# A mixture-of-experts block on one core: the next X loaded earlier, the experts' order turned, the branches of a last tile exchanged

## The chip, the core and the metric

The kernel runs on one NeuronCore of a Trainium2 chip, as one launch. Its engines are PE (TensorE matmul; PEld is its weight load), DVE (VectorE), ACT (ScalarE), POOL (GpSimd) and SP (SyncE, which here issues DMAs), and each takes its own list of instructions in order. The metric is device time in microseconds (us): 1101.23 us is the median of 3 runs before (1100.25 to 1102.68).

## The reference

One decoder layer over 1024 tokens of 1024 features: a gated spatial mixer and a sliding-window attention side by side, then a hierarchical mixture of experts, then a norm. The change touches the experts alone:

```python
# e_logits of the best of 4 groups; two experts of 4 inside it
combine = jnp.einsum("tk,tke->te", w_top, one_hot(expert_id, 16))
for e in range(16):
    hid = jax.nn.silu(t @ w_gate[e]) * (t @ w_up[e])      # 1024 -> 512
    out = out + combine[:, e:e+1] * (hid @ w_down[e])     # 512 -> 1024
```

Each token goes to two experts, so 2048 rows are shared out. By the reference's router on its own inputs the sixteen experts get 121, 82, 97, 130, 75, 39, 98, 76, 245, 162, 227, 134, 128, 113, 152 and 169 rows.

## The kernel before, in words

The dense part (some 648 us) ends with the routing, which writes every token's row into a queue in DRAM for each of its experts. Then the experts run one after the other, at places 0 to 15. Each matmul is made from three (high times high, high times low, low times high), so each weight must be split into a high part (ACT, L307) and a low part (DVE, L313 or L317). A granule is 128 x 1024 of raw weights, 512 KB: an expert has 12, k0 to k7 of gate and up (two DMAs of 256 KB) and k8 to k11 of down (one DMA of 512 KB). Granule g's raw buffer is loaded again with granule g + 9 when its low part is made (`load_others`, SP, L288). Fifteen split tiles go round in a ring.

An expert at place e has a main tile of its first 128 rows, and ahead of it, if it has more, a last tile: "half" (`half_tile`, up to 64 rows more) or "whole" (`whole_tile`). Both are in `last_tile` (L1574 ff.): an If on n > 128 (L1591), inside it an If on n <= 192 (L1595) with the half form, its Else with the whole one, and at the end the Else of the outer If with `fill(0)` and `fill(1)`, the first gate and up matmuls of the main tile, which in the other forms fill PE's waits. Places 0 and 15 have the whole form alone. All engines pass these branches, and tokens' counts are read at run time.

While PE works on the main tile of place e, ACT and DVE split granules of e + 1 at named steps (`ahead`, by the tables AHEAD_0 for e = 0, AHEAD_1 for e = 1, AHEAD for the others): "h5 l5" is high and low of granule k5. The steps of a main tile: ("k", 0 to 3) both halves of gate and up; ("f0", 5); then the first half's hidden rows (`hidden(0)`: Silu on ACT, L1388, product on DVE, L1389); ("f1", 5); their transposes on PE (`hidden_T`, L1395, which PE reaches in order) and the copies (L184 ACT, L185 DVE); ("f1", 7); the down projection (L1433) with ("y", 0), ("y", 1), ("y", 2) between its four steps. At ("y", 1) PE transposes the next expert's rows, X (L1344, from the buffer `xt_first`), and POOL copies their tail (L1337). At ("y", 2) SP loads X of place e + 2 into the same buffer (`first_rows`, L1328). At ("k", 2) SP loads the last rows of e + 1 (`last_rows`, L1475 to L1480, buffer `xt_last`; skipped where n does not ask for them, but issued).

SP and POOL run in the written order (`manual_schedule`). SP's order at the end of an expert is so that of the code in `ahead`: the loads that the lows of a step set off, then X. For places e > 1, ("y", 2) has one low, l11, which loads the next but one expert's k8; for e = 1 it has three, and for e = 0 seven.

`RANK_AT[p]` says which rank by count stands at place p (places 0 and 1 are fixed experts, the rest is sorted by `order_experts`). Before, the counts by place are 121, 82, 130, 128, 134, 113, 152, 98, 162, 97, 169, 76, 227, 75, 39, 245. With N for no last tile, H for half and W for whole, that is N N H N H N H N H N H N W N N W, which the trace shows in the tiles' names (2h, 4h, 6h, 8h, 10h, 12l, 15l). The last one's W is in the tail, which isn't changed.

Of the kernel before, what the change touches and what calls it, by code (L numbers as in the profile page):

```python
# [20 lines left out]
P = 128  # L21
H = P // 2
# [10 lines left out]
NE = 16  # L33
# [33 lines left out]

ORDER_AT = ("y", 2)

RANK_AT = [0, 1, 8, 9, 7, 10, 6, 11, 5, 12, 4, 13, 3, 14, 15, 2]  # L70

WARM = 42
WARM_ROUTE = 10
# [20 lines left out]
def kernel(  # L94
# [71 lines left out]
    def slot8(shape, dt, name):  # L166
        return slots.tile(shape, dt, tag="s8", name=name)

    def ps_mm(name):
        return ps.tile([P, 512], F32, tag="mm", bufs=4, name=name)  # L170

    def ps_tp(name):
        return ps.tile([P, 512], F32, tag="tp", bufs=2, name=name)
# [7 lines left out]
    def split_hi_lo(hi, lo, src, scale=None):  # L181

        if scale is None:
            nc.scalar.activation(hi, src, AF.Copy)  # L184
            return nc.vector.tensor_tensor(lo, src, hi, ALU.subtract)  # L185
        nc.scalar.activation(hi, src, AF.Copy, scale=scale)
        return nc.vector.scalar_tensor_tensor(lo, src, scale, hi, ALU.mult, ALU.subtract)
# [56 lines left out]
    def first_row(p):  # L244

        if p == len(first_rows_of):
            first_rows_of.append(
                nc.values_load(
                    base_i[0:1, p : p + 1], engines=[mybir.EngineType.SP],
                    min_val=0, max_val=(NE - 1) * CAP,  # L250
                )
            )
        return first_rows_of[p]

    class Granules:
# [63 lines left out]
        def fill(self, g):  # L319
            self.high(g)  # L320
            self.low(g)
# [1003 lines left out]
    def load_x(src, name, xt=None, **kw):  # L1325
        if xt is None:
            xt = moe.tile([P, XW], F32, tag="yt", bufs=1, name=f"xt_{name}")
        nc.sync.dma_start(xt, src, **kw)  # L1328
        return xt

    def transpose_x(xt, name, first=4, meta_src=None, xT=None, pts=None):

        if xT is None:
            xT = slot8([P, 2, KT, P], F32R, f"xT_{name}")
        meta = moe.tile([P, 8], F32, tag="meta", bufs=4, name=f"meta_{name}")
        if meta_src is None:
            nc.gpsimd.tensor_copy(meta, xt[:, D:XW])  # L1337
        else:
            nc.sync.dma_start(meta, meta_src)
        pts = pts or []  # L1340
        for q in range(len(pts), 2):
            pt = ps_tp(f"ps_xT_{name}_{q}")
            for k in range(4):
                nc.tensor.transpose(  # L1344
                    pt[:, k * P : (k + 1) * P], xt[:, (4 * q + k) * P : (4 * q + k + 1) * P], ident
                )
            pts.append(pt)
        pts = [pt[:].rearrange("p (k t) -> p k t", t=P) for pt in pts]
        pieces = [(0, first), (first, 4), (4, 8)] if first < 4 else [(0, 4), (4, 8)]
        for k0, k1 in pieces:  # L1350
            split_hi_lo(
                xT[:, 0, k0:k1, :], xT[:, 1, k0:k1, :], pts[k0 // 4][:, k0 % 4 : k0 % 4 + k1 - k0, :]
            )
        return xT, meta

    def gate_up_of(xT, e, accs):

        gu = [
            g[:].rearrange("p s (m f) -> p s m f", f=FF)
            for g in granules.split_tiles[12 * e : 12 * e + KT]  # L1360
        ]

        def gate_up(f, k):
            fs = slice(f * 256, (f + 1) * 256)
            mm3(
                accs[f], xT[:, 0, k, :], xT[:, 1, k, :], gu[k][:, 0, :, fs], gu[k][:, 1, :, fs],
                k == 0, k == KT - 1,
            )

        return gate_up  # L1370
# [90 lines left out]
    def first_rows(e):  # L1461
        return load_x(xs_d[bass.ds(first_row(e), P), :], f"{e}", xt_first)

    def count_of(e):
        return nc.values_load(cnt_i[0:1, e : e + 1], min_val=0, max_val=S)

    def last_rows(e, n):

        start = nc.values_load(
            start_i[0:1, e : e + 1], engines=[mybir.EngineType.SP],  # L1470
            min_val=0, max_val=NE * CAP - P,
        )
        meta = moe.tile([P, 8], F32, tag="meta2", bufs=1, name=f"meta2_{e}")
        for part in (slice(0, H), slice(H, P)):
            nc.sync.dma_start(meta[part], xs_d[bass.ds(start + H, H), D:XW], cond=n > P)  # L1475
        xt = xt_last
        nc.sync.dma_start(xt[H:P], xs_d[bass.ds(start + H, H), :], cond=n > P)

        both = n > (P if e in WHOLE else P + H)
        nc.sync.dma_start(xt[0:H], xs_d[bass.ds(start, H), :], cond=both)  # L1480
        return n, xt, meta
# [88 lines left out]
    def hint(label, stays):  # L1570

        tc.mark_branch_hint_location(label, hint=stays, engines=[mybir.EngineType.PE])

    def last_tile(e, n, xlast, mlast, fill):  # L1574

        banks = {"bank": ps_sc, "bank_T": ps_tp}
        xT = xT_last  # L1580

        def beside(step):
            if step == ("f1", 7):
                fill(1)

        def whole_tile():
            xl, ml = transpose_x(xlast, f"{e}l", 4, None, xT)
            fill(0)
            expert_tile(xl, ml, e, dup_i[:, e : e + 1], f"{e}l", beside, **banks)

        with tc.If(n > P, label=f"more{e}") as more:  # L1591
            if e in WHOLE:
                whole_tile()
            else:
                with tc.If(n <= P + H) as few:  # L1595
                    half_tile(xlast, xT, mlast, e, f"{e}h", fill)
                with few.Else():
                    whole_tile()
        with more.Else():
            fill(0)  # L1600
            fill(1)
# [88 lines left out]
    n = count_of(0)  # L1690
# [16 lines left out]
    for e in range(NE - 1):  # L1707
        accs = [ps_mm(f"ps_gu_{e}_{f}") for f in range(2)]
        gate_up = gate_up_of(xT, e, accs)


        first = range(12 * e + 12, 12 * e + 12 + (FIRST if e > 1 else 0))

        def fill(k):
            gate_up(0, k)
            gate_up(1, k)
            if k == 0:
                for g in first:
                    granules.split(g)

        last_tile(e, n, *lasts, fill)
        got = {}

        def ahead(step):
            if e == 0 and step == ORDER_AT:
                next(ordering)
            if step == ("k", 2):
                got["n"] = last_rows(e + 1, count_of(e + 1))
            if step == ("f1", 5):
                if e + 2 < NE:  # L1730
                    hint(f"more{e + 1}", got["n"][0] > P)
                else:
                    got["most"] = nc.values_load(most_i[0:1, 0:1], min_val=0, max_val=S)
                    hint("many", got["most"] > 2 * P)
            if step == ("y", 1):
                got["x"] = transpose_x(xnext, f"{e + 1}", xT=xT)
            for part in (AHEAD_0, AHEAD_1, AHEAD)[min(e, 2)].get(step, "").split():
                g = 12 * (e + 1) + int(part[1:])
                if part[0] == "h":
                    granules.high(g)  # L1740
                else:
                    granules.low(g)
                    granules.load_others(g)
            if step == ("y", 2) and e + 2 < NE:
                got["next"] = first_rows(e + 2)

        expert_tile(xT, meta, e, None, f"{e}", ahead, accs=accs, done=2)
        n, *lasts = got["n"]
        xT, meta = got["x"]
        xnext = got.get("next")  # L1750
# [5 lines left out]
    e = NE - 1  # L1756
# [161 lines left out]
def _constants():  # L1918
# [14 lines left out]
    misc[16:32] = np.arange(16) * CAP  # L1933
    misc[32:48] = RANK_AT
    return {"c_bucket": onehot, "c_maskrow": maskrow, "c_misc": misc}
# [33 lines left out]
```

## Time and profile before

| | us |
|---|---|
| median of 3 runs | 1101.23 |
| lowest and highest run | 1100.25, 1102.68 |
| the profiled execution | 1100.0 |
| its span, first to last instruction | 1098.3 |
| mean granted TensorE clock in it | 0.975 |

The profile is of one execution of its own, 1.2 us under the median; its span is 1.7 us less than its time. In the views, idle time stands in brackets behind an instruction with what ended it, and a wait is told as who waited for whom. An expert's time is best read from one transpose of X to the next, since PE passes this point once for each place.

### The profile page before, as it was taken

The numbers are of one execution on the slowest core, as the hardware profiler recorded it, in microseconds if no ns is written. First come the engines' busy times: TensorE is split into PE (matmuls) and PEld (weight loads), VectorE is DVE, ScalarE is ACT, GpSimd is POOL, SyncE is SP. The second block draws the span as 40 slices with busy tenths as digits, with TensorE's granted clock in tenths as the row PEclk, the third lists the DMA queues.
The fourth block names the chain that finished last, engine by engine and source line by source line (L and its number), as shares of the span: only waits on it lengthen the run. The fifth ranks groups of instructions, "written<-read, shape, count | busy, mean of one in ns | idle before, by whom it ended". The sixth has DMA issues, their size and how long they took to land. (4 is left out here: it accounts for less than half of the span.)

```text
span 1098.3 us, 15559 instructions
## 1 busy us (share of the span) xinstructions
PE 1029.1 (94%) x4823; PEld 828.0 (75%) x4823; DVE 719.9 (66%) x1585; ACT 606.9 (55%) x1014; POOL 102.3 (9%) x128
## 2 busy tenths in 40 slices
PE   7999899999999999999999988899989999999893
PEld 6778788788888888887888876677767777777682
DVE  6752577775358455775455778786868686838735
ACT  5543465543356365554344445686857686847643
POOL 4001000000004000000000122011111101010020
PEclk9998999999999999999999989899999999999897
DMA  7433545545137413323555646979898998978854
GB/s 246 117 101 109 168 159 169 184 138 192 41 114 277 147 39 103 90 58 87 182 192 182 213 181 210 349 242 323 276 296 264 292 292 275 302 237 297 262 215 191
DMA packets 125477, 214.46 MB, mean 195 GB/s; under 512 B 11563, under 2 KB 58731, under 8 KB 125360
## 3 DMA queue, kind: packets, MB, share of 16 engines
q1 hardware_dynamic: 112016, 176.58, 48.5%
q0 software_dynamic: 7200, 21.20, 7.1%
q10 hardware_dynamic: 6144, 15.27, 3.7%
q8 instruction: 56, 0.92, 0.3%
q14 instruction: 61, 0.50, 0.1%
HBM read 185.46 MB, written 37.63 MB: 203 GB/s over the span
## 5 line engine op out<-in xcount | busy, mean ns | idle before, releaser
L313 DVE SCALAR_TENSOR_TENSOR w_e<-raw_e,g2T,w_e 128x1024 fp32r<-128x1024 f32 x127 | 156.7, 1281 | 24.2 <-ACT w_e L307 18.0
L307 ACT ACTIVATE w_e<-raw_e,g2T 128x1024 fp32r<-128x1024 f32 x127 | 138.0, 1143 | 17.1 <-PE ps_gu L209 5.5
L207 PE MATMUL ps_gu<-w_e,xT 128*128 128x512 f32 x256 | 104.2, 407 | 2.4 <-issue 2.1
L1433 PE MATMUL ps_y<-w_e,hT 128*128 128x512 f32 x384 | 102.7, 412 | 0.4 <-ACT hT L184 0.4
L209 PE MATMUL ps_gu<-w_e,xT 128*128 128x512 f32 x256 | 101.6, 397 | 0.0
L208 PE MATMUL ps_gu<-w_e,xT 128*128 128x512 f32 x256 | 101.3, 396 | 0.0
L1433 PEld LDWEIGHTS ps_y<-w_e,hT 128*128 128x128 f32 x384 | 71.9, 195 | 17.0 <-ACT hT L184 2.1
L317 DVE TENSOR_TENSOR w_e<-raw_e,w_e 128x1024 fp32r<-128x1024 f32 x63 | 75.0, 1218 | 0.0
L307 ACT ACTIVATE w_e<-raw_e 128x1024 fp32r<-128x1024 f32 x63 | 65.8, 1055 | 3.9 <-DMA raw_e<-in_expert_w_down_dram 3.5
L207 PEld LDWEIGHTS ps_gu<-w_e,xT 128*128 128x128 f32 x256 | 48.6, 190 | 13.7 <-issue 2.8
L209 PEld LDWEIGHTS ps_gu<-w_e,xT 128*128 128x128 f32 x256 | 48.6, 190 | 11.4
L208 PEld LDWEIGHTS ps_gu<-w_e,xT 128*128 128x128 f32 x256 | 48.7, 190 | 9.9
L575 PE MATMUL ps_gv<-w_gv,xh 128*128 128x512 f32 x192 | 48.4, 406 | 3.9 <-ACT xh L184 2.4
L209 PE MATMUL ps_o<-w_wo,ms 128*128 128x512 f32 x128 | 51.4, 403 | 0.0
L208 PE MATMUL ps_o<-w_wo,ms 128*128 128x512 f32 x128 | 51.2, 400 | 0.0
L207 PE MATMUL ps_o<-w_wo,ms 128*128 128x512 f32 x128 | 51.0, 399 | 0.0
L207 PE MATMUL ps_ga<-xh,w_ga 128*128 128x512 f32 x128 | 50.8, 397 | 0.0
L208 PE MATMUL ps_ga<-xh,w_ga 128*128 128x512 f32 x128 | 50.7, 396 | 0.0
L209 PE MATMUL ps_ga<-xh,w_ga 128*128 128x512 f32 x128 | 50.6, 396 | 0.0
L208 PE MATMUL ps_gb<-xh,w_gb 128*128 128x512 f32 x128 | 50.5, 395 | 0.0
L209 PE MATMUL ps_gb<-xh,w_gb 128*128 128x512 f32 x128 | 50.5, 395 | 0.0
L207 PE MATMUL ps_gb<-xh,w_gb 128*128 128x512 f32 x128 | 50.5, 395 | 0.0
(539 smaller groups left out, 2374.4 us busy)
## 6 DMA issues: line engine op xcount, KB each, us to landing
raw_e<-in_expert_w_gate_dram SPq DMA_DIRECT2D x127, 256.0 KB
raw_e<-in_expert_w_up_dram SPq DMA_DIRECT2D x127, 256.0 KB
raw_e<-in_expert_w_down_dram SPq DMA_DIRECT2D x63, 512.0 KB
xs_d<-zero ACTq DMA_DIRECT2D x16, 516.0 KB
xt_last<-xs_d SPq DMA_DIRECT2D x32, 258.0 KB
raw_ga<-in_w_in_dram SPq DMA_DIRECT2D x16, 512.0 KB
raw_gb<-in_w_in_dram SPq DMA_DIRECT2D x16, 512.0 KB
raw_wo<-in_w_out_dram SPq DMA_DIRECT2D x16, 512.0 KB
```

The lines of the kernel that those rows point to most:

```text
L207: nc.tensor.matmul(acc, lhi, rhi, start=start, stop=False)
L208: nc.tensor.matmul(acc, lhi, rlo, start=False, stop=False)
L209: return nc.tensor.matmul(acc, llo, rhi, start=False, stop=stop)
L307: nc.scalar.activation(self.split_tiles[g][:, 0, :], self.raw[g], AF.Copy, **scale)
L313: nc.vector.scalar_tensor_tensor(w[:, 1, :], raw, g2T[:, k : k + 1], w[:, 0, :], ALU.mult, ALU.subtract)
L317: nc.vector.tensor_tensor(w[:, 1, :], raw, w[:, 0, :], ALU.subtract)
L575: nc.tensor.matmul(accs[i], xh[a][k // 4][:, k % 4, t], gs[j][:, b, k % 2, :], start=k + a + b == 0, stop=k == KT - 1 and b == 1,)
L1433: nc.tensor.matmul(ys[nh], hT[:, a, k, :], dn[k][:, b, nh * 512 : (nh + 1) * 512], start=k + i == 0, stop=k == FK - 1 and i == 2,)
```

## The change

Three edits. (1) At ("y", 2) the load of X for place e + 2 is issued ahead of the granules' loads of that step instead of behind them. (2) `RANK_AT` is turned: the counts by place become 121, 82, 128, 130, 113, 134, 98, 152, 97, 162, 76, 169, 75, 227, 39, 245, that is N N N H N H N H N H N H N W N W. (3) The inner If of `last_tile` asks n > 192 and has the whole form first, the half form in its Else.

```diff
-RANK_AT = [0, 1, 8, 9, 7, 10, 6, 11, 5, 12, 4, 13, 3, 14, 15, 2]
+RANK_AT = [0, 1, 9, 8, 10, 7, 11, 6, 12, 5, 13, 4, 14, 3, 15, 2]
...
             if e in WHOLE:
                 whole_tile()
             else:
-                with tc.If(n <= P + H) as few:
+                with tc.If(n > P + H) as many:
+                    whole_tile()
+                with many.Else():
                     half_tile(xlast, xT, mlast, e, f"{e}h", fill)
-                with few.Else():
-                    whole_tile()
...
             if step == ("y", 1):
                 got["x"] = transpose_x(xnext, f"{e + 1}", xT=xT)
+            if step == ("y", 2) and e + 2 < NE:
+                got["next"] = first_rows(e + 2)
             for part in (AHEAD_0, AHEAD_1, AHEAD)[min(e, 2)].get(step, "").split():
                 g = 12 * (e + 1) + int(part[1:])
                 if part[0] == "h":
                     granules.high(g)
                 else:
                     granules.low(g)
                     granules.load_others(g)
-            if step == ("y", 2) and e + 2 < NE:
-                got["next"] = first_rows(e + 2)
```

## Rows read from the trace of the kernel before

**Rows 1.** The page's first part: busy us, share of the span, instructions.

```profile
PE 1029.1 (94%) x4823; PEld 828.0 (75%) x4823; DVE 719.9 (66%) x1585; ACT 606.9 (55%) x1014; POOL 102.3 (9%) x128
```

**Rows 2.** Windows from X to X, places 1 to 4 and 12 to 14; columns in line two.

```profile
core 0: us, PE busy (x) PEld busy (x) DVE busy (x) ACT busy (x) POOL busy (x), PEclk, DMA share, GB/s
668.30:694.40 26.10, 19.88 (x84) 15.24 (x83) 24.16 (x40) 17.83 (x22) 6.48 (x2) 0.93 0.80 243
694.40:729.20 34.80, 33.16 (x147) 25.40 (x146) 25.34 (x37) 24.39 (x34) 5.18 (x5) 0.95 0.80 285
729.20:748.40 19.20, 18.23 (x87) 14.60 (x85) 17.04 (x21) 16.26 (x20) 1.77 (x2) 1.00 1.04 347
748.40:780.00 31.60, 31.11 (x147) 24.32 (x145) 22.39 (x35) 20.80 (x30) 6.22 (x4) 1.00 0.80 261
...
956.80:995.30 38.50, 36.48 (x171) 29.21 (x170) 20.38 (x29) 20.03 (x28) 4.81 (x5) 1.00 0.74 224
995.30:1015.30 20.00, 19.04 (x92) 15.34 (x91) 16.68 (x21) 15.84 (x20) 1.75 (x2) 1.00 0.98 340
1015.30:1039.70 24.40, 19.15 (x79) 15.13 (x79) 17.98 (x21) 16.72 (x21) 1.85 (x2) 0.86 0.92 293
```

**Rows 3.** Waits of PE, 648 to 1045 us: us in total, times, longest.

```profile
PE ps_hT L1395 <- DVE hid L1389: 17.8, 13, 5.2
PE ps_xT L1344 <- DMA xt_first<-xs_d: 3.8, 1, 3.8
PE ps_gu L207 <- issue: 2.1, 1, 2.1
PE ps_xT_12l L1344 <- DMA xt_last<-xs_d: 1.9, 1, 1.9
PE ps_xT_6h L1494 <- DMA xt_last<-xs_d: 1.6, 1, 1.6
...
PE ps_xT_10h L1494 <- DMA xt_last<-xs_d: 1.0, 1, 1.0
...
PE ps_xT_8h L1494 <- DMA xt_last<-xs_d: 0.4, 1, 0.4
```

**Rows 4.** Timeline of PE at places 3 and 14: start, us, instruction, [idle before].

```profile
743.47 0.44 PE L1395 MATMUL ps_hT<-ident,hid 128*128 128x128 f32 x2 [0.97 <-DVE hid L1389]
...
745.14 1.56 PE L1433 MATMUL ps_y<-w_e,hT 128*128 128x512 f32 x6
...
1033.05 0.69 PE L1395 MATMUL ps_hT<-ident,hid 128*128 128x128 f32 x2 [5.25 <-DVE hid L1389]
```

**Rows 5.** Windows of a stall's clock and of an idle DMA; columns as Rows 2.

```profile
1030.10:1036.90 6.80, 3.85 (x10) 3.13 (x11) 4.64 (x6) 4.39 (x7) 0.19 (x1) 0.50 1.03 370
673.00:676.00 3.00, 3.00 (x15) 2.43 (x14) 2.79 (x11) 3.00 (x4) 0.00 (x0) 1.00 0.04 13
```

**Rows 6.** Timeline of SP: the loads of place 0's last steps and X of place 2.

```profile
670.02 0.33 SPq L288 DMA_DIRECT2D raw_e<-in_expert_w_up_dram  x1
...
683.79 0.33 SPq L1328 DMA_DIRECT2D xt_first<-xs_d  x1
```

**Rows 7.** Timeline of DVE: lows of place 2's weights around X's split.

```profile
690.47 3.68 DVE L313 SCALAR_TENSOR_TENSOR w_e<-raw_e,g2T,w_e 128x1024 fp32r<-128x1024 f32 x3
695.45 1.29 DVE L185 TENSOR_TENSOR xT<-ps_xT,xT 128x512 fp32r<-128x512 f32 x2 [1.30 <-ACT xT L184]
...
698.18 4.62 DVE L317 TENSOR_TENSOR w_e<-raw_e,w_e 128x1024 fp32r<-128x1024 f32 x4
```

**Rows 8.** Timeline of ACT at places 3 and 13: highs of k8.

```profile
742.96 1.05 ACT L307 ACTIVATE w_e<-raw_e 128x1024 fp32r<-128x1024 f32 x1
743.95 0.39 ACT L184 ACTIVATE hT<-ps_hT 128x256 fp32r<-128x256 f32 x1
...
1009.70 1.06 ACT L307 ACTIVATE w_e<-raw_e 128x1024 fp32r<-128x1024 f32 x1 [0.57 <-DMA raw_e<-in_expert_w_down_dram]
```

**Rows 9.** Timeline of POOL at the same places: the copy that waits for X.

```profile
744.58 0.19 POOL L1337 COPY meta<-xt_first 128x8 f32<-128x8 f32 x1 [8.73 <-DMA xt_first<-xs_d]
...
1012.21 0.19 POOL L1337 COPY meta<-xt_first 128x8 f32<-128x8 f32 x1 [10.30 <-DMA xt_first<-xs_d]
```

**Rows 10.** DMA queues in 817 to 823 us: packets, MB, share.

```profile
q8 instruction: 2, 0.03, 2.3%
```

## The prediction

> **What bounds the kernel now.** I read first the page's busy shares [rows 1]: PE is busy 94% of the span, so time can come only from PE's idle stretches, or from matmuls at the lower clock. The windows from X to X [rows 2] then show each place by itself. A place with no last tile after one that has one (N) takes 19.2 us, with DVE busy 17.0 of it and the DMA engines full (share 1.04); one with a half tile (H) takes 31.6 us with DVE at 22.4 and DMA at 0.80. So N lives on a little more than DVE and DMA can give, and H lets both recover. The reader should see the three odd rows. Place 1, the second N in a row, takes 26.1. Place 2 takes 34.8, though its form is H. Place 14, again the second N in a row, takes 24.4, where place 13 took 20.0. The list of PE's waits [rows 3] names what stands behind it: 17.8 us on the product of the hidden rows (5.2 of it once), 3.8 us once on X, 2.1 us once on "issue", and four waits of 0.4 to 1.9 us on the last rows. The timeline [rows 4] puts the 5.25 us at 1027.8 to 1033.05, in place 14; an ordinary N has 0.97 there. [...]
>
> **The order of few and many.** It moves one N from the end (W N N becomes N W N) to the front (N N H N becomes N N N H). At the end, places 12 to 14 take 38.5 + 20.0 + 24.4 = 82.9 us now [rows 2]. With an N after an H (19.2), the whole form (38.5) and an N after it (20.0) it is 77.7: **5.2 us less**. What is late next there is the isolated N's 0.97 us wait, which is in the 19.2.
>
> At the front, places 1 to 3 take 26.1 + 34.8 + 19.2 = 80.1 us now. Afterwards place 1 loses the wait for X (below), 26.1 - 3.75 = 22.35, so X of place 2 is transposed at about 690.6. Place 2 is then a third N. DVE works through three lows to 694.15 [rows 7], X's split (1.29, 695.4) and five lows more at about 1.2 each (3 in 3.68, 4 in 4.62): 701.5. The order of the steps puts seven lows of place 3's weights (k0 to k6) ahead of place 2's first hidden product: 701.5 + 7 x 1.2 + 0.4 = 710.3. PE needs it earlier: in place 14 the stall began 12.5 us after X (1015.3 [rows 2] to 1027.8), here 690.6 + 12.5 = 703.1, and some 1.5 more as X's split waits for DVE, 704.6. So it waits 5.7 us, much as in place 14 with 5.25, and its clock falls behind it likewise. In place 14 X followed 1039.7 - 1033.05 = 6.65 us after the stall: here X of place 3 comes at 710.3 + 6.65 = 717.0, and place 2 takes 26.4. Place 3 is an H, 31.6. Sum 22.35 + 26.4 + 31.6 = 80.35, against 80.1: **0.25 us more**. Place 2 isn't shown as an N; I bound it below by place 14 (24.4, so 1.75 less than 80.1) and above by its 26.4 with 3.4 us more, what a second stretch like 1030.1 to 1036.9 costs, 6.8 us at half rate [rows 5] (29.8, so 3.65 more). I keep 26.4, as it comes out of DVE's rows. The five H and W between are the same experts with the same neighbours, one place later.
>
> **X ahead of the granules.** It adds and removes no instruction. At place 0, X now passes seven granules' loads on SP: 683.79 becomes the slot behind 670.02 [rows 6]. Its buffer is free by then (X of place 1 is transposed from 668.3 on [rows 2]), and in 673 to 676 the DMA engines are nearly idle, share 0.04 [rows 5], so X lands some 15 us before PE wants it and costs the granules nothing. The 3.75 us of place 1 go. What is late next is DVE: its X split started at 695.45 after 1.30 us of idling [rows 7], and only these 1.3 us are really gained there, the rest is the wait at 704.6 in the sum above. At place 1 X passes three granules, which DVE's list in the sum above reaches later than they land. At later places it passes one, k8, in a full DMA queue. There the two change places: k8's data come when X's did. In place 3 ACT splits k8 at 742.96 [rows 8] and X is there at 744.58 [rows 9]: k8 about 1.6 us later. In place 13 it is 1009.70, where ACT already waits 0.57 us for k8, against 1012.21: 2.5 us later. The copy of the hidden rows stands behind k8's high on ACT (743.95, done 744.34 [rows 8]), and PE needs it at 745.14 [rows 4]: 0.8 us of slack. So PE loses about 0.8 us in an N, up to 1.7 in the last one. In four of the five pairs N to H or W, PE waits for the last rows at the end of the N anyway (1.6, 0.4, 1.0, 1.9 [rows 3]); their place in SP's queue isn't moved, so this wait shrinks by what PE is later. I take 0.8 once for the pair without it and 1.2 for place 14: **2.0 us more**. Bounds: 0, if the queue isn't full at that point, and 6 x 1.6 = 9.6, if there were no slack and no wait to hide in.
>
> **The whole form first.** No work is added. Before, a half form is fallen into and left by a jump over the whole one; afterwards it is entered by that jump. One of the five jumps left PE 2.1 us idle on "issue" [rows 3], with instruction packets on q8 in the same 6 us [rows 10]. That goes: **2.07 us less**. The new jump at the head isn't shown for a half form. For the whole one it is: at place 12 PE jumps over the half form, and the idle time there is put down to the last rows alone [rows 3]. Behind the branch PE has the last two down steps (12 matmuls) queued. I take a third of one miss, **0.7 us**; bounds 0 and 5 x 2.07 = 10.35.
>
> [...]
>
> **Sum.** -5.2 + 0.25 + 2.0 - 2.07 + 0.7 = -4.3 us against the profiled execution: 1100.0 - 4.3 = 1095.7. The median of the runs shown is 1.2 above that execution, so 1096.9, **1097.0 us**.
>
> **The rivals.**
>
> *Given back at the front.* Place 2 as the third N costs its upper bound, 29.8: DVE and DMA have had no H to recover in, and PE's clock falls twice. For it: places 1 and 14 [rows 2]; against: at place 2 the weights it multiplies are nearly all split when it starts. Then -4.3 + 3.4 = -0.9: 1100.3, no change.
>
> *All parts cheap.* k8's delay hides in the last rows' waits, the jumps don't miss, and place 2 is like place 14: -5.2 - 1.75 - 2.07 = -9.0: 1092.2.
>
> *The jump at the head misses* (slower). At each of the five half forms PE waits for its instructions; the place is the first transpose of the last rows, the price 2.07 us each, in place of the 0.7: -4.3 - 0.7 + 10.35 = +5.35, 1106.6. It ends slower from about four misses of this size that the waits for the last rows don't cover. Against it: place 12 [rows 3].
>
> *X in front of k8 stops every N* (slower). 9.6 in place of 2.0: +3.3, 1104.5. It decides from about 1.4 us lost in each of the six N; the slack of 0.8 us [rows 4, 8] speaks against it.
>
> *X isn't earlier*, since its buffer is held. POOL's copy of X for place 1 was done before place 0's end, so I see no reason; it would cost the 1.3 us of DVE: 1098.3.
>
> **How the numbers follow.** Chances: forecast (1094 to 1099) 0.52; given back at the front 0.20; all cheap 0.12; jump misses 0.06; k8 0.06; X not earlier 0.04. A measurement of this kernel can tell about 0.2%, 2.2 us, from no change, so faster is below 1099.0 and slower above 1103.4. Faster: all cheap, X not earlier and most of the forecast, 0.65. Same: the front and the forecast's upper edge, 0.24. Slower: both slower rivals less what they fall short by, 0.11. The range for 8 in 10 reaches down to the cheap case, 1092.5, and up over the front's rival, 1102.5, and leaves the slower ones out.
>
> **What would show it.** Right: place 2 some 26 us from X to X with one wait of 5 to 6 us on the hidden product; no wait of PE for X at 690; place 14 near 20 us and the granted clock at full level there; ACT's high of k8 about 1.6 us later against its neighbours in each N, and shorter waits for the last rows; no "issue" behind a half form. Wrong: a wait on "issue" ahead of the last rows' transposes in several places, a place 2 of 29 us or more, or an N that has become longer than 20.5 us.

## The result, and the profile after

The kernel after takes 1093.09 us (median of 8 runs, 1091.8 to 1098.1) against 1101.03 us before, measured beside it: ratio 0.9936, interval 0.9916 to 0.9956, some 7 us faster. The forecast was 1097.0 with a range of 1092.5 to 1102.5: the sign and the range held, the range by 0.6 us, and the size was 4 us short. The profiled execution took 1093.03 us, its span is 1091.3 us, 7.0 less than before. The ratios in this document leave out one of the twelve runs of "X alone", which took 1266.8 us at a granted clock of 0.75.

The page's first part for after, to set beside [rows 1]: the busy times are the same, so what went is idle time.

```profile
PE 1028.8 (94%) x4823; PEld 827.6 (76%) x4823; DVE 719.6 (66%) x1585; ACT 606.2 (56%) x1014; POOL 111.8 (10%) x128
```

The windows of after from X to X, for places 1 to 4 and 10 to 14 (columns as in [rows 2]), and below them, from the timeline of PE, the wait in place 14:

```profile
666.80:689.00 22.20, 19.72 (x85) 15.39 (x84) 20.51 (x38) 15.83 (x21) 6.52 (x2) 0.92 0.82 260
689.00:717.60 28.60, 19.94 (x85) 15.64 (x84) 23.62 (x26) 21.87 (x26) 4.56 (x2) 0.88 1.00 356
717.60:749.10 31.50, 31.16 (x147) 24.35 (x146) 22.46 (x35) 20.76 (x30) 6.02 (x4) 1.00 0.73 242
749.10:768.60 19.50, 18.49 (x87) 14.58 (x86) 17.21 (x21) 16.20 (x20) 2.54 (x2) 1.00 1.03 348
...
903.80:924.50 20.70, 18.40 (x87) 14.56 (x85) 17.07 (x21) 16.09 (x20) 2.32 (x2) 1.00 1.01 343
924.50:955.90 31.40, 30.93 (x146) 24.30 (x145) 22.41 (x35) 20.77 (x30) 6.04 (x4) 1.00 0.80 263
955.90:975.50 19.60, 18.49 (x87) 14.56 (x86) 17.13 (x21) 16.18 (x20) 1.96 (x2) 1.00 1.03 348
975.50:1012.80 37.30, 36.58 (x170) 29.09 (x168) 20.28 (x29) 20.05 (x28) 4.79 (x5) 1.00 0.72 231
1012.80:1032.40 19.60, 18.52 (x87) 14.57 (x85) 17.17 (x21) 16.19 (x20) 1.99 (x2) 1.00 1.01 336
...
1027.16 0.44 PE L1395 MATMUL ps_hT<-ident,hid 128*128 128x128 f32 x2 [0.99 <-DVE hid L1389]
```

Three things are to be seen. Place 14 takes 19.6 us at the full clock, where before it took 24.4 at 0.86; its wait on the hidden product, 5.25 us before [rows 4], is 0.99. Place 2, now the third N in a row, is the dearest N of the list, 28.6 us with the DMA engines full (1.00) and PE's clock at 0.88. And place 10 takes 20.7 us, where an N took 19.2.

The waits of PE in after, to set beside [rows 3] (total us, times, longest):

```profile
PE ps_hT L1395 <- DVE hid L1389: 21.6, 14, 8.4
PE ps_y L1433 <- ACT hT L184: 2.9, 3, 1.2
PE ps_xT_13l L1344 <- DMA xt_last<-xs_d: 0.6, 1, 0.6
...
PE ps_xT_9h L1494 <- DMA xt_last<-xs_d: 0.2, 1, 0.2
```

The wait for X and the wait on "issue" are gone, and the four on the last rows (4.9 us) have shrunk to 0.8. New are 2.9 us in the down projection (`ps_y`), and one wait of 8.4 us on the hidden product in place of one of 5.2.

Read in three stretches, after less before, from the first transpose of X in each place: places 1 to 3 82.5 - 80.2 = +2.2; places 4 to 11 206.8 - 208.4 = -1.6; places 12 to 14 76.5 - 82.9 = -6.4; the tail +0.3. That is -5.5. The other 1.5 us lie ahead of X of place 1, in code that is not edited: this point lay between 665.8 and 668.7 us in the twelve profiles of this study, and differed by 1.7 between the two of the kernel before and by 1.4 between the two of after. So it is chance of a single execution, and of the profile's 7.0 us only these 5.5 belong to the edits.

### The profile page after: what moved, and what is told of

It reads as the page before. It is cut to its first block, busy times and chain, and to the rows that moved or that the text cites. A ratio compares the mean times of both kernels' runs of the same rounds, so it can differ in the third digit from the quotient of the medians.

```text
span 1091.3 us, 15560 instructions
## 1 busy us (share of the span) xinstructions
PE 1028.8 (94%) x4823; PEld 827.6 (76%) x4823; DVE 719.6 (66%) x1585; ACT 606.2 (56%) x1014; POOL 111.8 (10%) x128
## 5 line engine op out<-in xcount | busy, mean ns | idle before, releaser
L208 PE MATMUL ps_o<-w_wo,ms 128*128 128x512 f32 x128 | 51.2, 400 | 0.0
```

The source lines that it names most:

```text
L208: nc.tensor.matmul(acc, lhi, rlo, start=False, stop=False)
```

## The experiments

All kernels in one view: stretches between the first transposes of X in the trace, by place, in us; "issue" is PE's waits of that name from X of place 1 to X of place 15. The stretches of a row come from one profile, its ratio from many runs; the profile need not be a typical one of its kernel:

| kernel | order | early X | first form | 1 | 2 | 3 | 4 to 11 | 12 to 14 | X 1 to end | issue | ratio to before, interval |
|---|---|---|---|---|---|---|---|---|---|---|---|
| before | old | no | half | 26.2 | 34.8 | 19.2 | 208.4 | 82.9 | 430.4 | 2.1 | 1 |
| before, again | old | no | half | 25.6 | 35.6 | 19.2 | 207.3 | 82.8 | 429.7 | 4.2 | 1.0016, 0.9992 to 1.0040 |
| order alone | turned | no | half | 24.7 | 25.0 | 32.6 | 207.2 | 76.6 | 425.2 | 3.3 | 0.9947, 0.9926 to 0.9968 |
| X alone | old | yes | half | 22.3 | 38.5 | 19.9 | 208.6 | 79.6 | 427.8 | 2.0 | 0.9997, 0.9974 to 1.0020 |
| whole alone | old | no | whole | 24.7 | 37.0 | 19.2 | 204.1 | 82.3 | 426.1 | 0 | 0.9953, 0.9931 to 0.9974 |
| order, X | turned | yes | half | 22.3 | 28.9 | 32.2 | 208.4 | 78.1 | 428.8 | 2.5 | 0.9957, 0.9940 to 0.9974 |
| after | turned | yes | whole | 22.3 | 28.7 | 31.5 | 206.8 | 76.5 | 424.9 | 0 | 0.9936, 0.9916 to 0.9956 |
| after, again | turned | yes | whole | 21.5 | 29.6 | 31.5 | 206.1 | 78.8 | 426.6 | 0 | 0.9935, 0.9911 to 0.9959 |
| order, whole | turned | no | whole | 24.9 | 25.1 | 31.5 | 204.7 | 76.0 | 421.2 | 0 | 0.9900, 0.9877 to 0.9923 |
| X at place 0 | turned | place 0 | whole | 21.5 | 26.2 | 31.5 | 205.3 | 77.4 | 421.2 | 0 | 0.9903, 0.9878 to 0.9927 |
| no whole form | turned | no | half only | 25.3 | 24.9 | 31.5 | 203.9 | 78.9 | 423.8 | 0 | 0.9908, 0.9881 to 0.9935 |
| two lows left out | turned | place 0 | whole | 21.5 | 26.3 | 31.7 | 204.4 | 77.3 | 420.1 | 0 | 0.9907, 0.9879 to 0.9935 |

### The three edits, each alone, and the kernel before once more

**The order alone.**

```diff
-RANK_AT = [0, 1, 8, 9, 7, 10, 6, 11, 5, 12, 4, 13, 3, 14, 15, 2]
+RANK_AT = [0, 1, 9, 8, 10, 7, 11, 6, 12, 5, 13, 4, 14, 3, 15, 2]
```

> The kernel before with the turned order alone; X's load stays behind the granules' loads and the half form stays first. The changed kernel spent 82.4 us on places 1 to 3 (forecast 80.35), with one wait of 8.35 us on the hidden product in place 2. Theory A (the forecast's: place 2 waits for DVE's lows): the 3.75 us wait for X returns in place 1, of which DVE gives back all but 1.3, so places 1 to 3 take about 80.35 + 1.3 = 81.7; the end gains 5.2 to 6.3; sum -3.6 to -4.7, 1096.3 to 1097.4. Theory B (place 2 waits for the granules k5 and k6 of place 3, which land late because X, 0.5 MB, stands ahead of k6 in a full DMA queue): without X ahead of it k6 lands about 1.5 us sooner, places 1 to 3 take about 80.9; sum -4.4 to -5.5, 1095.5 to 1096.6. The trace tells them apart better than the time: by A, ACT's high of k6 is made long after k6 landed; by B, within 0.2 us of it.

Measured: 1095.11 us, ratio 0.9947, about -5.8 us, a little more than either theory gave. The three end places gain 82.9 - 76.6 = 6.3 us, and places 1 to 3 take 82.3 us, more than either theory gave (place 3 has 32.6 where after has 31.5, with a wait of 0.94 us on "issue"). Of the theories on place 2, the rows decide. With X late, ACT (first) runs seven highs on end without a wait, and DVE (second) seven lows; the product follows at once:

```profile
699.44 7.38 ACT L307 ACTIVATE w_e<-raw_e,g2T 128x1024 fp32r<-128x1024 f32 x7
706.73 0.37 ACT L1388 ACTIVATE hid<-ps_gu 128x256 f32<-128x256 f32 x1
708.22 1.15 ACT L307 ACTIVATE w_e<-raw_e,g2T 128x1024 fp32r<-128x1024 f32 x1 [1.13 <-DMA raw_e<-in_expert_w_up_dram]
...
700.68 8.46 DVE L313 SCALAR_TENSOR_TENSOR w_e<-raw_e,g2T,w_e 128x1024 fp32r<-128x1024 f32 x7 [0.21 <-issue]
709.06 0.41 DVE L1389 TENSOR_TENSOR hid<-hid,ps_gu 128x256 f32<-128x256 f32 x1
```

The same stretch of after (ACT, DVE, then SP, where L1328 is the load of X of place 3 and the two below it are k6's gate and up):

```profile
697.84 6.53 ACT L307 ACTIVATE w_e<-raw_e,g2T 128x1024 fp32r<-128x1024 f32 x6
708.33 1.15 ACT L307 ACTIVATE w_e<-raw_e,g2T 128x1024 fp32r<-128x1024 f32 x1 [3.97 <-DMA raw_e<-in_expert_w_up_dram]
...
699.49 7.26 DVE L313 SCALAR_TENSOR_TENSOR w_e<-raw_e,g2T,w_e 128x1024 fp32r<-128x1024 f32 x6
709.51 1.28 DVE L313 SCALAR_TENSOR_TENSOR w_e<-raw_e,g2T,w_e 128x1024 fp32r<-128x1024 f32 x1 [2.76 <-ACT w_e L307]
710.71 0.41 DVE L1389 TENSOR_TENSOR hid<-hid,ps_gu 128x256 f32<-128x256 f32 x1
...
697.91 0.33 SPq L1328 DMA_DIRECT2D xt_first<-xs_d  x1
698.57 1.18 SPq L288 DMA_DIRECT2D raw_e<-in_expert_w_gate_dram  x1
699.94 0.33 SPq L288 DMA_DIRECT2D raw_e<-in_expert_w_up_dram  x1
```

In after, ACT idles 3.97 us until k6 has landed, and DVE 2.76 us behind it. PE's wait on the product is 8.35 us in after and 3.59 with the order alone. So theory B holds for after: its place 2 waits for k6, which stands behind X in SP's list. The other profiles say the same: the three with X ahead of k6 have this wait at 8.4 to 8.8 us, the five in the turned order with X behind k6 at 2.3 to 5.5.

**X alone.** Order and forms stay as before.

```diff
+            if step == ("y", 2) and e + 2 < NE:
+                got["next"] = first_rows(e + 2)
             for part in (AHEAD_0, AHEAD_1, AHEAD)[min(e, 2)].get(step, "").split():
...
-            if step == ("y", 2) and e + 2 < NE:
-                got["next"] = first_rows(e + 2)
```

> The kernel before with X's load ahead of the granules' loads alone; order and forms as before. Theory A (the forecast's): the 3.75 us wait for X in place 1 goes, 1.3 us of it for good, and k8's delay costs about 2.0 us net in the N places: +0.7, 1101.7, no change. Theory B (k8's delay only takes the place of the waits for the last rows, as the changed kernel's N places and H places together were as long as before): -1.3 to -3.75, 1097.3 to 1099.7.

Measured: 1100.95 us, ratio 0.9997: no change. The interval, some -3 to +2 us, holds theory A and most of B, so the time doesn't tell them apart. The trace shows a give-back from one place to the next. Place 1 loses its wait for X, 26.2 to 22.3; place 2 grows from 34.8 to 38.5. Its rows on PE (the last rows' transposes, and the first product with them):

```profile
692.90 0.68 PE L1494 MATMUL ps_xT_2h<-ident,xt_last 64*128 64x64 f32 x8 [0.98 <-DVE xT L185]
...
699.20 0.96 PE L1513 MATMUL ps_gu_2h<-w_e,xT_last 128*128 128x512 f32 x3 [4.04 <-DVE xT_last L185]
```

PE gets X 3.8 us sooner and then waits 0.98 + 4.04 us for DVE, in all 5.0 us; before it waited 3.75 for X and 1.26 for DVE, also 5.0. Places 1 and 2 together take 60.8 us against 61.0 and 61.2 in the two profiles of before. In this profile places 12 to 14 are 3.3 us shorter too (place 14's wait on the hidden product is 0.99 here as well, with 2.10 in its down projection), but it was the fastest of the kernel's runs (1095.36), and the median shows no such gain.

**The whole form first, alone.**

> The kernel before with the whole form ahead of the half one alone. Theory A (the forecast's): the wait of 2.07 us on issue behind a half form goes and a third of one comes at the head: -1.4, 1099.6. Theory B (the one wait on issue was no property of the form's place, but happens now and then): 0, 1101.0. Rival C (the jump at the head misses at each half form): +8, 1109.

```diff
-                with tc.If(n <= P + H) as few:
-                    half_tile(xlast, xT, mlast, e, f"{e}h", fill)
-                with few.Else():
+                with tc.If(n > P + H) as many:
+                    whole_tile()
+                with many.Else():
+                    half_tile(xlast, xT, mlast, e, f"{e}h", fill)
```

Measured: 1095.86 us, ratio 0.9953, about -5.2 us, three to four times theory A's 1.4 and against B. Places 4 to 11 take 204.1 us against 208.4 and 207.3, no wait on "issue" is left, and none appears at the heads, so rival C falls. From X of place 1 to the end the profile is 3.6 to 4.3 us shorter than the two of before.

**The kernel before, once more.**

> The kernel before, word for word, as a control with a profile of its own. Every theory: 0. What it tells: whether the 2.07 us wait on issue behind the half form of place 6 comes again (forecast: yes, by its place; rival: not, or elsewhere), and by how much the dense part's length differs between two profiled executions of one kernel (the changed kernel's was some 1.5 us shorter up to X of place 1, in code that isn't edited; if it is chance, this profile should lie 1 to 2 us off the first one as well).

Measured: 1100.96 us, ratio 1.0016, as expected. Its profile goes some way to explain the run above. The wait on "issue" behind place 6's half form came again, with another one behind place 4's that the first profile did not have:

```profile
PE ps_gu L207 <- issue: 4.2, 3, 2.0
...
767.88 0.39 PE L207 MATMUL ps_gu<-w_e,xT 128*128 128x512 f32 x1 [1.78 <-issue]
```

The five profiles with the half form first have such a wait of 1.8 to 2.1 us behind the half forms of place 6 (before), 4 and 6 (before, again), 4 (X alone), 5 (order alone) and 5 (order, X), and in the last two a shorter one at place 3 (0.94 and 0.57). None of the six with the whole form first has one. In four of the five the trace's record of PE's jump at the end of the half form lasts 4.2 to 4.3 us at place 6 or 5 (0.2 to 0.6 us at the others), of which the twelve matmuls queued ahead of it hide some 2. Here are PE's branches of the inner If in before and, below, in after, as their number and their shortest, median and longest time in ns:

```profile
L1595 PEldq COMPARE_BRANCH  x12: 67/188/4302, 694.6 to 980.0; - x12
...
L1595 PEldq COMPARE_BRANCH  x12: 70/289/328, 717.8 to 997.5; - x12
```

The packets of the instruction queue q8, of 16 KB each, separate the half forms with a wait from those without. At the eight with one, no such packet began inside the form; the next began 1.4 to 1.9 us behind the start of the jump, and PE's wait ended 3.8 to 4.4 us behind it. At the other 17 half forms of these five profiles a packet began 0.2 to 7.7 us ahead of the jump. Place 4 shows both. Before, again, its jump starts at 763.81 and the packet at 765.5; before, the packet starts at 763.7 and the jump at 765.52. The packets in 763.8 to 767.9 (before, again), and in 761.5 to 765.5 (before):

```profile
q8 instruction: 1, 0.02, 1.6%
...
q8 instruction: 1, 0.02, 1.5%
```

So the packets that the prediction took for a sign [rows 10] say nothing by being there, since before has some at nearly every place; their time tells. Why one is late at some half forms is not shown.

### The edits in pairs

> The changed kernel without its first edit: the turned order and the whole form first, X's load behind the granules' loads as before. The first four runs gave -6 for the order alone, -5 for the whole form alone, about 0 for X alone, against -8 for all three. Theory A (X's load ahead of k8, and of k6 at place 1, costs more than it brings): the N places go back from 19.5 to 20.7 to 19.2 (4.3 us in five of them), the waits for the last rows come back with some 2 us, place 2 loses its wait for k6 (3.7 us) and place 1 gets its wait for X back (2.4): -3.5 against the changed kernel, about 1089.5. Theory B (X's load costs nothing in this order either, the other two edits overlap): 1093, as the changed kernel.

The edit, against after:

```diff
-            if step == ("y", 2) and e + 2 < NE:
-                got["next"] = first_rows(e + 2)
             for part in (AHEAD_0, AHEAD_1, AHEAD)[min(e, 2)].get(step, "").split():
...
                     granules.load_others(g)
+            if step == ("y", 2) and e + 2 < NE:
+                got["next"] = first_rows(e + 2)
```

Measured: **1090.55 us, ratio 0.9900**, with after at 1095.52 beside it: theory A. It is the lowest ratio of the table, though two other kernels that compute the whole, X at place 0 and no whole form, lie within its interval. Windows of places 1, 2, 10 and 11:

```profile
668.40:693.20 24.80, 19.92 (x85) 15.29 (x84) 23.12 (x40) 17.83 (x22) 6.57 (x2) 0.93 0.79 256
693.20:718.20 25.00, 20.53 (x86) 16.33 (x85) 21.35 (x24) 20.09 (x24) 2.89 (x3) 0.86 1.01 365
...
902.80:922.20 19.40, 18.33 (x87) 14.54 (x85) 17.07 (x21) 16.22 (x20) 1.76 (x2) 1.00 0.99 338
922.20:954.30 32.10, 30.90 (x146) 24.29 (x144) 22.46 (x35) 20.86 (x31) 5.11 (x4) 1.00 0.83 271
```

Place 10 takes 19.4 in place of 20.7, place 11 32.1 in place of 31.4 (the last rows' wait is back). Why shows in ACT's high of k8 and PE's down step there, first with X behind k8, then in after, with X ahead of it:

```profile
917.06 0.44 PE L1395 MATMUL ps_hT<-ident,hid 128*128 128x128 f32 x2 [1.07 <-DVE hid L1389]
917.45 1.06 ACT L307 ACTIVATE w_e<-raw_e 128x1024 fp32r<-128x1024 f32 x1 [0.79 <-DMA raw_e<-in_expert_w_down_dram]
918.84 1.66 PE L1433 MATMUL ps_y<-w_e,hT 128*128 128x512 f32 x6
```

```profile
918.07 0.44 PE L1395 MATMUL ps_hT<-ident,hid 128*128 128x128 f32 x2 [1.08 <-DVE hid L1389]
919.75 1.06 ACT L307 ACTIVATE w_e<-raw_e 128x1024 fp32r<-128x1024 f32 x1 [2.01 <-DMA raw_e<-in_expert_w_down_dram]
921.13 1.66 PE L1433 MATMUL ps_y<-w_e,hT 128*128 128x512 f32 x6 [1.22 <-ACT hT L184]
```

Against the transposes of the hidden rows, k8's high starts at +0.39 without and at +1.68 with X ahead: 1.3 us later, and PE waits 1.22 us, since the copy of the hidden rows stands behind this high on ACT. Counted in the same way, k8's high in the five N of places 4 to 12 is 0.9 to 1.9 us later in after, 1.2 on average. These five N are 4.0 us longer together, and the waits for the last rows give back 1.4.

**X early at place 0 alone.** Against after:

```diff
-            if step == ("y", 2) and e + 2 < NE:
+            if step == ("y", 2) and e == 0:
                 got["next"] = first_rows(e + 2)
...
                     granules.load_others(g)
+            if step == ("y", 2) and e + 2 < NE and not (e == 0):
+                got["next"] = first_rows(e + 2)
```

> The changed kernel with X's load ahead of the granules' loads at place 0 alone; from place 1 on it stands behind them as before. Theory A (place 2's wait in the changed kernel was for k6, behind X in SP's list): ACT's high of k6 at place 2 no longer waits for a DMA, DVE runs its seven lows through and ends them near 708, the wait on the hidden product is 4 to 5 us in place of 8.35, X of place 3 comes at 714 to 715 in place of 717.4; with the N places back at 19.2: about 1088.5, or 1 us under the kernel without any early X. Theory B (DMA work is only shifted: an X loaded earlier at place 0 makes another granule late): as without any early X. If DVE bounded place 2 all along (the forecast's): 8.35 us stays.

Measured: 1091.44 us, ratio 0.9903. By the front theory A holds: ACT's high of k6 waits 0.17 us for its landing in place of 3.97, PE's wait on the product falls from 8.35 to 5.50, place 2 from 28.7 to 26.2, and X of place 3 comes 47.8 us after X of place 1, in place of 51.0. The kernel without any early X needs 49.9. (The same stretch is 51.0 to 51.2 in the three turned profiles with X ahead of k6, 49.7 to 50.1 in the three with X late, 47.8 in both with X early at place 0 alone.) ACT's high of k6, DVE's seven lows and the window of place 2:

```profile
706.87 1.15 ACT L307 ACTIVATE w_e<-raw_e,g2T 128x1024 fp32r<-128x1024 f32 x1 [0.17 <-DMA raw_e<-in_expert_w_up_dram]
...
701.56 8.45 DVE L313 SCALAR_TENSOR_TENSOR w_e<-raw_e,g2T,w_e 128x1024 fp32r<-128x1024 f32 x7
...
690.50:716.70 26.20, 19.85 (x86) 15.44 (x85) 24.18 (x28) 21.96 (x26) 3.07 (x2) 0.93 1.01 367
```

But these 2.2 us are gone by the end (421.2 us from X of place 1 to the end in both), so in the time theory B's "as without any early X" is what came. The end of the trace shows some of where: place 13's wait for the last rows is 1.84 us here and 0.53 there. This wait has values from 0.5 to 2.2 in the twelve profiles, so one pair of executions doesn't settle whether the early X of place 0 is given back or hit by chance.

**The half form first, with order and X.** Against after:

```diff
-                with tc.If(n > P + H) as many:
-                    whole_tile()
-                with many.Else():
+                with tc.If(n <= P + H) as few:
                     half_tile(xlast, xT, mlast, e, f"{e}h", fill)
+                with few.Else():
+                    whole_tile()
```

> The changed kernel without its third edit: half form first, its end jumping over the whole one. Theory A (each half form's exit can leave PE without instructions, in the profiles of the four kernels so far that have it 1, 2, 1 and 2 times in five with about 2 us each, and never in the two that enter it by a jump): +3 to +5 against the changed kernel, 1096 to 1098, with one or more waits of 1.7 to 2.1 us on issue behind half forms, and the single times spread over 8 us or more. Rival (the whole-first gain of 5 us was another thing, as the placing of code): 1093 with such waits, or +5 without.

Measured: 1097.06 us (1093.8 to 1101.3), ratio 0.9957, with after's 0.9935 beside it: 2.4 us slower by the ratios, whose intervals overlap, and 1.5 by the medians measured side by side, less than theory A gave. The waits on "issue" are back, 1.97 us behind place 5's half form and 0.57 at place 3. The first costs more than its length: the granted clock falls to 0.67 behind it, and place 5 takes 35.7 us where after takes 31.4. The windows of the wait and of the 3.5 us behind it:

```profile
789.70:791.70 2.00, 0.04 (x1) 0.00 (x0) 1.40 (x2) 1.98 (x4) 0.00 (x0) 1.00 0.89 356
791.70:795.20 3.50, 3.49 (x11) 2.80 (x12) 2.85 (x3) 2.23 (x3) 2.41 (x2) 0.67 0.33 108
```

**After, once more.**

> The changed kernel word for word, as a control beside the other three: 1093, place 2 with its wait of about 8 us behind k6's high, no wait on issue behind a half form.

Measured: 1095.52 us, ratio 0.9935 (0.9936 the first time): the ratio is stable. Its wait in place 2 is 8.74 us, behind 3.88 us of ACT's waiting for k6, and no "issue" stands behind a half form.

### The jump, and DVE in place 2, by themselves

**No whole form where there is a half one.**

```diff
             if e in WHOLE:
                 whole_tile()
+            elif e != 13:
+                half_tile(xlast, xT, mlast, e, f"{e}h", fill)
             else:
```

> The turned order without any early X (the kernel of 1090.5) with the whole form's code left out at the places that have a half form, for these counts of rows: PE has nothing to jump over, neither at the head of a half form nor at its end; place 13 keeps both forms. Theory A (the waits on issue belong to the jump from a half form's end over the whole form's code, and the jump at its head is hidden behind the queued down steps): no wait on issue behind a half form, and 1090.5 within a microsecond. Rival B (the head's jump costs something that no idle row shows, 0.33 us each as its record lasts): 1089. Rival C (the waits belong to where code lies, whatever jumps there are): the code is moved here too, so waits of about 2 us come at one or two half forms, 1093 to 1095.

Measured: 1091.12 us, ratio 0.9908, with the 0.9900 of order and whole within the interval. No wait on "issue" at all: theory A. The jump over the whole form, at the head of a half form that comes second, costs nothing that can be measured against a half form that stands alone; the code jumps over `fill` at the end of both.

**Two of the seven lows left out**, on the kernel with the early X at place 0 (the low parts of k0 and k1 of place 3's weights are left out of the computation).

```diff
         def low(self, g):
...
+            if g in NO_LOW:
+                nc.vector.memset(w[:, 1, 0:8].bitcast(F32), 0.0)
+                return
```

> The kernel with the early X at place 0 alone (1091.4), with the low parts of k0 and k1 of place 3's weights left out (2 of the seven lows that DVE makes ahead of place 2's hidden product; its output lacks them). Theory A (with k6 landed in time, DVE's seven lows bound place 2, as the forecast held): DVE is done 2.4 us sooner, the product then waits for ACT's Silu behind its high of k6, so the wait of 5.5 us falls to 3.5 to 4.0 and X of place 3 comes 1.5 to 2 us sooner after X of place 1 (47.8 in place of 47.8 + ...: from 47.8 to about 46). Rival B (ACT or the DMA bound it just as much): 47.8 stays. For the whole time: by A 1089.5 to 1090, if the later places don't give it back through their waits for the last rows.

Measured: 1089.84 us, ratio 0.9907, against 0.9903 with the two lows; the absolute time would fit theory A, but the kernel before, measured beside it, was faster too (1099.31). X of place 3 comes 47.85 us after X of place 1, against 47.77. PE's wait on the product falls only from 5.50 to 4.97, not to the 3.5 to 4.0 of theory A, and 0.45 us of waiting in the down projection are new. Rival B holds. ACT and DVE in this stretch (the lines of this kernel are numbered up to five higher), and the window of place 2:

```profile
702.48 1.15 ACT L309 ACTIVATE w_e<-raw_e,g2T 128x1024 fp32r<-128x1024 f32 x1 [0.78 <-DMA raw_e<-in_expert_w_up_dram]
...
708.82 1.15 ACT L309 ACTIVATE w_e<-raw_e,g2T 128x1024 fp32r<-128x1024 f32 x1 [2.32 <-DMA raw_e<-in_expert_w_up_dram]
...
700.69 2.48 DVE L318 SCALAR_TENSOR_TENSOR w_e<-raw_e,g2T,w_e 128x1024 fp32r<-128x1024 f32 x2 [0.96 <-ACT w_e L309]
703.66 3.88 DVE L318 SCALAR_TENSOR_TENSOR w_e<-raw_e,g2T,w_e 128x1024 fp32r<-128x1024 f32 x3 [0.49 <-ACT w_e L309]
707.46 0.41 DVE L1394 TENSOR_TENSOR hid<-hid,ps_gu 128x256 f32<-128x256 f32 x1
...
688.60:714.90 26.30, 20.04 (x86) 15.23 (x85) 22.00 (x28) 21.89 (x26) 3.07 (x2) 0.94 1.01 364
```

DVE is busy 22.0 us in it, against 24.2 above, and idles 0.96 and 0.49 us behind ACT's highs. These wait for landings, k4's for 0.78 us and k7's for 2.32 (2.34 with the two lows), and the DMA engines are full in both windows (share 1.01). So even where no X stands ahead of k6, taking 2 us of work from DVE gives nothing: the DMA is a bound of place 2 beside it.

## Why the prediction was right, and where its sizes were off

**The end** was forecast at -5.2 us and gave -6.3 (order alone: places 12 to 14). The mechanism was right: place 14 is no longer a second N, its 5.25 us wait is 0.99, its clock is full, and with the order alone this comes without any early X. What the forecast priced with an N after the whole form at 20.0 came as 19.2 (order alone) and 19.6 (after).

**The front**, forecast +0.25, gave +2.2. Place 1 was right (22.35 forecast, 22.3). Place 2 was forecast at 26.4 with a wait of 5.7 us, and took 28.7 with 8.35. The step that failed is the sentence that at place 1 "X passes three granules, which DVE's list in the sum above reaches later than they land". DVE's list was as held. Counted from X of place 1 (667.9 before, 666.4 in after), its seventh low would have been done at 41.6 us in after (six were done at 706.75, and one takes 1.28), where the forecast has 42.0 (709.9). But ACT's high of k6 began only at 41.9 us (708.33), when k6 had landed behind the 0.5 MB of X in a full queue (DMA share 1.00 in place 2); the seventh low came behind it, and the product began at 44.3 us. With X early at place 0 alone, k6's high begins at 38.2 us and the product at 41.2, the wait is 5.50, place 2 takes 26.2, and places 1 to 3 take 79.3 us in place of 82.5: in these two profiles the step was worth 3.2 us. The 5.50 is close to the 5.7, but not for the reason given alone: the run with two lows left out shows that DVE was not the only bound.

The gain of place 1 that the forecast put at 1.3 us is, in the old order, nothing (X alone), and in the turned order, place 0 alone, 2.2 us up to X of place 3, which the time does not show.

**X ahead of k8**, forecast +2.0 us. The step was right in kind and nearly in its amount: k8 comes 1.3 us later in place 10, and 1.2 on average, where 1.6 was forecast, the slack of 0.8 is used up, PE waits up to 1.2 us in an N, and the waits for the last rows shrink from 2.1 to 0.8 us in total (order and whole against after). Net the two profiles of after against order and whole give +1.5 to 2.1 us in places 4 to 11 and +0.5 to 2.7 in places 12 to 14; against the other profiles with X late in these places (203.9 to 205.3, and 77.3 to 78.9) the first stays above zero and the second does not. The forecast let one pair pay only, and held the others covered by waits of 0.4 to 1.9 us; the measured cover was smaller, 1.4 us against the 4.0 that five N lost. With place 2's part, the first edit costs 4 to 5 us in the turned order (0.9936 and 0.9935 against 0.9900; 1095.52 against 1090.55 side by side).

**The whole form first**, forecast -2.07 + 0.7 = -1.4, gave -5.2 alone and, by the ratios, -5.2 in the turned order without early X and -2.4 with it. The sign was right; the term was mis-sized, in part because it was taken from one execution. The rows behind the forecast showed one wait on "issue" in five half forms; the other profile of the same kernel has two. And the 0.7 for misses at the head, an estimate of a third of one such wait, was nothing: no such wait in six profiles with five heads each. How 5.2 us come out of 2 to 4 us of waits in a profile is not fully settled: a lower clock behind some of them, as the 0.67 in place 5 above, is part of it, and profiled executions with fewer such waits than the median one are possible but not shown: the one profiled is the fastest of its kernel's runs for X alone (1095.36, median 1100.95) and for before, again (1097.60, median 1100.96).

The waits stand at the eight ends of half forms named above, where the q8 packet comes 1.4 to 1.9 us behind the jump. None stands at the head, where a jump over the same whole form is taken in 0.32 to 0.33 us in after's profile. The rival of a miss at each head is refuted: 1106.6 against 1093.09, and no wait at any head. Why head and end differ, and why half forms of places 3 to 6 were hit, not in every profile, and those of place 2 and of 7 to 11 never, no run shows. The code calls `hint(f"more{e + 1}", ...)` for PE ahead of the outer If and nothing of the kind ahead of the inner one, and no run varied that.

**The rivals.** "Given back at the front" named the right place: 28.7 is within 1.1 us of its 29.8. Its cause, DVE and the DMA without an H to recover in, was at most part of it: the DMA was full (share 1.00), but DVE idled 2.76 us, and with X behind k6 the same third N takes 24.9 to 26.3. "All parts cheap" was right on the jumps and the end, wrong on k8 and on place 2, and the time came out near its 1092.2 all the same. With the measured sizes the sum is -6.3 (end) + 2.2 (front) + 2.6 (k8: 2.1 + 0.5) - 5.2 (whole form alone) = -6.7, against the 5.5 of the profile's edited places and the 7 of the ratio. It sets profiles of one execution beside a ratio of medians, so it tells the size to 1 or 2 us at best. So the range held partly by luck, because errors cancel: the front was 2 us dearer than forecast, the end 1.1 and the jumps up to 3.8 cheaper. "X isn't earlier" is out: PE has no wait for X in after. "X in front of k8" came in kind, not at the 1.6 for each N that it needed to end slower.

**What should show it.** Right: no wait for X at 690, place 14 near 20 us at full clock, k8's high later, shorter waits for the last rows, no "issue" behind a half form. Wrong: place 2, 28.7 us in place of some 26, and 29.6 in the second profile of after, past the 29 that was named as a sign; and one N in each profile (place 10 with 20.7, place 12 with 21.0) is past the 20.5 us that was named as a sign against the step on k8.

## What to carry to other kernels

Here a load of 516 KB, moved ahead in a queue that was full (DMA share 1.00 at place 2, 1.01 at place 10), moved other loads back, k6's high by 3.7 us and k8's by 1.3; the gain counts only if the load that is passed has the slack for it, to be asked separately at each place where the code stands (at place 0 the DMA engines were nearly idle, share 0.04 [rows 5], at place 1 the queue held k6, later k8). A stall that occurs "once" in a profile should be read in a second profile of the same kernel before it is priced. When changes come together, run each alone and each left out: here leaving out one edit of three saved 4 us in the order that the others had made, and adding it to the old order changed nothing.

## What was not expected of the hardware

- PE's jump out of the half form lasted 4.2 to 4.3 us at one half form of each order (place 6 in the old order, place 5 in the turned one), in four of the five profiles that have this jump, and 0.2 to 0.6 us at the others. At places 3 and 4 PE idled 0.6 to 2.0 us though the record of the jump was 0.2 us. Counted from the start of the jump to the end of the wait, both kinds last 3.8 to 4.4 us.
- A PE idle for about 2 us kept its clock in three profiles (granted clock 1.00 in the 3.5 us after it: before, before again, order alone) and lost it in two (0.57 with X alone, 0.67 with order and X).
- A wait of 2.15 us for the last rows at place 13, in the kernel with no whole form at the half ones' places, was followed by a granted clock of 0.55, and the place took 40.5 us; where the same wait was 0.53 us (order and whole) the clock stayed at 1.00 and it took 37.3, and where it was 1.84 us (X at place 0) it took 38.6, longer by no more than the wait. The 3.5 us behind the long one:

```profile
979.00:982.50 3.50, 3.50 (x13) 3.04 (x14) 1.59 (x3) 2.47 (x4) 1.26 (x3) 0.55 1.07 379
```
